# Sums of weights kept in DRAM for half of the Strassen products of a hybrid decoder layer's down-projection

## The chip, the cores and the metric

The kernel runs on one core of one Trainium2 chip. The metric is the device time of one execution in microseconds. Times are medians of several runs; a profile is one execution.

## What is computed

One decoder layer on x (256 tokens, 2048 columns, fp32): token mixing by two groups of attention heads, then a channel mixer. The change is in the channel mixer:

```python
h = rmsnorm(x, pre_ffn_g)                         # 256 x 2048
u = causal_dwconv(h @ w_up, conv_w, conv_b)       # w_up 2048 x 11264, width 3 along tokens
gate, val = jnp.split(u, 2, axis=-1)              # 256 x 5632 each
y = (gelu(gate) * val) @ w_down                   # w_down 5632 x 2048
x = x + rmsnorm(y, post_ffn_g)
```

## The kernel before

All of it is written by hand for one core. A matrix of fp32 numbers goes through TensorE (PE) in two parts: a high part (`whi`, `act.copy` on ScalarE, ACT) and a low part (`wlo`, the rest, `dve.tensor_tensor` on VectorE, DVE), and a product takes three matmuls: high x high, high x low, low x high. Weights are loaded by SP into `raw` buffers of 512 KB (five of them), split by ACT and DVE into `whi` and `wlo` (five of each), and used by PE.

The channel mixer works in two halves of the 5632 columns. For each half:

- **w_up** (`proj_T`, 11 groups g of 256 columns, gate and value): 16 matmuls high, 32 low and so on through the four units of a projection, in the order `LONG`: high of units 0 and 1, low of 0 to 3, high of 2 and 3. A `tick()` follows each of the 8 steps of a projection, 16 in a group; work put off with `later` runs at ticks. After each projection `conv` evacuates the two banks: a copy on ACT (`cs`), a sum on DVE (`u`), a product on GpSimd (POOL, `u` x `rowf`), an activation on ACT and two DVE operations, then gelu on ACT for the gate, a DVE product for the value. The result y (256 tokens of two k-tiles) is split into a tile G. For the first groups, the "sevens" below also need sums of y's quarters (`s`, on POOL, split into `sums`).
- **w_down** (four column blocks of 512, in pairs n = 0 and 2): the 22 k-tiles of the half are taken two at a time, u = 0 to 10. A **four** (`four`) is the plain product of two k-tiles and one column block for both token tiles, 12 matmuls of 512 columns; two of them cover a pair of blocks. A **seven** (`seven`) does the same 2 x 2 blocks with Strassen's seven products instead of eight, 21 matmuls in place of 24. It loads two rows of weights (`top` and `low`, 512 KB each), makes four sums of weight blocks in place on DVE (128x512 each) and four more splits. Its first three products stand before the fours of the same step, the other four (`others`) behind them; four of the seven go to banks of their own (`shared`), which `fold` adds up into y_sb after the last seven. `SEVENS` says at which steps of each half and pair sevens stand: 5, 5, 4 and 2 of them. At the end of a pair `down` evacuates the four banks of the plain products (DVE, 128x512 each).
- The last pair of half 1 (`tail`) does block 2 in its loop and block 3 in closing products: 512 columns for the first token tile, two halves of 256 columns (`b1`) for the second.

PE's instructions stand in the order of the code. Those of ACT, DVE, POOL and SP are put in order by the framework when it builds the program, by its own plan of when each can run, except where a manual schedule or `keep_in_program_order` fixes them. Each engine takes its instructions one after the other, a DMA that it issues included: a wait in front of one holds all behind it.

Lines of before that the steps touch: L119 and L122 (split of a weight unit), L263 and L270 (PE high and low of w_up), L857 to L864 (conv), L929 (gelu), L937 (gate x value), L949 to L952 (POOL's sums), L978 (products of w_down), L1005 to L1008 (a seven's weight sums), L967 (`down`), L1036 to L1050 (`fold`), L285 (`b1`).

Of the kernel before, what the change touches and what calls it, by code (L numbers as in the profile page):

```python
# [17 lines left out]
P = 128  # L18
# [9 lines left out]
SEVENS = (((0, 1, 2, 3, 4), (0, 1, 2, 3, 4)), ((0, 1, 3, 4), (0, 2)))  # L28
# [5 lines left out]
def hybrid_layer(ctx: ExitStack, tc: tile.TileContext, x, pre_mix_g, w_in, b_forget, sinks,  # L34
# [22 lines left out]

    def tick():
        now[0] += 1
        for f in todo.pop(now[0], []):  # L60
            f()
# [759 lines left out]
    with tc.tile_pool(name="ffn", bufs=1) as fp:  # L821
# [30 lines left out]
        def conv(b, ch, dst_tag):  # L852
# [6 lines left out]
            y = fp.tile([P, 256], F32, tag=dst_tag, bufs=4, name=dst_tag)  # L859
# [6 lines left out]
            return y  # L866

# [41 lines left out]
        for half in range(2):  # L909
# [3 lines left out]
            if half:  # L913
                sums = main.tile([P, 4096], F32R, tag="x", name="sums")
            for g in range(FHALF // 2):
# [10 lines left out]
                gates = []  # L926
                for m in range(2):
                    y = conv(bg[m], c0 // P + m, "yg")
                    act.activation(y, y, AF.Gelu_apprx_tanh)  # L929
                    gates.append(y)  # L930
# [4 lines left out]
                for m in range(2):  # L935
                    y = conv(bv[m], 44 + c0 // P + m, "yv")
                    dve.tensor_tensor(y, y, gates[m], op=ALU.mult)  # L937
                    ys.append(y)
                if g < most:
                    if half == 0 and g == 0:  # L940
                        for t in range(2):
                            sp.dma_start(x_dram[t * P:(t + 1) * P, :], x_sb[:, t, :])
                        sums = main.tile([P, 4096], F32R, tag="x", name="sums")
# [3 lines left out]
                    if not half:  # L947
                        s1 = a21
# [7 lines left out]
                if g < most:  # L956
                    w = 384 + 128 * half
                    split(*(sums[:, i * w:i * w + w] for i in (2 * g, 2 * g + 1)), s[:, :w])
# [31 lines left out]
            def seven(n, u, last, banks, opened):  # L990
# [3 lines left out]
                top, low = [w_load(w_rows(w_down, k + i, 1, n * 512, 1024), 1, 1024, raw=x)[0]  # L994
                            for i, x in enumerate((None, None if tail else fp.tile(
                                [P, UNIT], F32, tag="gbc", bufs=2, name="low")))]
                b11, b12, b21, b22 = (x[:, i:i + 512] for x in (top, low) for i in (0, 512))
                w = 384 + 128 * half
                s2, s3, s4, s1 = [[sums[:, v * w + i * P:v * w + i * P + P]
                                   for v in (2 * u, 2 * u + 1)] for i in range(4)]  # L1000
                if not half:
                    s1 = parts_of(u * 2, 1)
                (w11,) = split_into(w_parts(UNIT, held=False), top, 1)
                w21, w22 = split_into(w_parts(UNIT, held=False), low, 2)
                dve.tensor_tensor(b11, b12, b11, op=ALU.subtract)  # L1005
                dve.tensor_tensor(b12, b22, b12, op=ALU.subtract)
                dve.tensor_tensor(b22, b22, b11, op=ALU.subtract)
# [188 lines left out]
```

## Time and profile before

| | |
|---|---|
| Median of 3 runs | 1057.03 us (1056.82 to 1058.18) |
| The profiled execution | 1056.84 us |
| its span, first to last instruction | 1055.1 us |
| granted TensorE clock | 0.999 |
| moved by DMA | 207.09 MB, mean 196 GB/s |
| w_up, one group of two projections | 21.88 us |

In the profile PE is TensorE's matmuls and PEld its weight loads, which overlap them. L119 is line 119 of the kernel. "out<-in" names tiles without their buffer numbers. A row of a group ends in busy us, mean ns of one, and the idle time before it with what ended it. `<-issue` stands where the profile shows no releaser. SPq and ACTq are the DMAs that SP and ACT issue.

### The profile page before, as it was taken

The numbers are of one execution on the slowest core, as the hardware profiler recorded it, in microseconds if no ns is written. First come the engines' busy times: TensorE is split into PE (matmuls) and PEld (weight loads), VectorE is DVE, ScalarE is ACT, GpSimd is POOL, SyncE is SP. The second block draws the span as 40 slices with busy tenths as digits, with TensorE's granted clock in tenths as the row PEclk, the third lists the DMA queues.
The fourth block names the chain that finished last, engine by engine and source line by source line (L and its number), as shares of the span: only waits on it lengthen the run. The fifth ranks groups of instructions, "written<-read, shape, count | busy, mean of one in ns | idle before, by whom it ended". The sixth has DMA issues, their size and how long they took to land.

```text
span 1055.1 us, 16356 instructions
## 1 busy us (share of the span) xinstructions
PE 1044.0 (99%) x5914; PEld 909.2 (86%) x5914; DVE 833.1 (79%) x1337; ACT 639.8 (61%) x1099; POOL 256.2 (24%) x287
## 2 busy tenths in 40 slices
PE   9999999999999999999999999999999999999996
PEld 7889988888889888888888887888888888888886
DVE  5989877886468887887768999877778677788994
ACT  7777757767557666665655655546566565565651
POOL 3253236341122332321212000003432121200031
PEclk9999999999999999999999999999999999999999
DMA  8645666545875766656664666775657665647583
GB/s 292 194 122 180 181 188 204 176 157 161 299 239 179 228 202 198 199 182 200 199 193 149 193 204 202 239 217 183 191 173 214 199 197 184 192 147 231 175 266 125
DMA packets 161597, 207.09 MB, mean 196 GB/s; under 512 B 6860, under 2 KB 131052, under 8 KB 160620
## 3 DMA queue, kind: packets, MB, share of 16 engines
q1 hardware_dynamic: 161196, 205.65, 62.7%
q8 instruction: 46, 0.75, 0.3%
q10 hardware_dynamic: 320, 0.40, 0.1%
q14 instruction: 35, 0.29, 0.1%
HBM read 201.68 MB, written 4.21 MB: 195 GB/s over the span
## 4 chain that ended last, share of the span: by engine, by line
PE 96%; DVE 2%; DMA 1%; issue 0%; ACT 0%; SPq 0%; DVEq 0%; POOLq 0%; ACTq 0%
PE bank_acc L263 21%; PE bank_acc L978 16%; PE bank_att L263 15%; PE bank_acc L285 13%; PE bank_acc L270 11%; PE bank_att L270 8%; PE bank_att L978 4%; PE bank_att L285 1%; PE bank_att L451 1%; PE bank_att L486 1%; PE bank_att L495 1%; PE bank_acc L882 1%; PE bank_acc L226 1%; DMA x_in<-in_x_dram 1%; PE bank_att L226 1%; DVE wlo L122 0%
## 5 line engine op out<-in xcount | busy, mean ns | idle before, releaser
L122 DVE TENSOR_TENSOR wlo<-raw,whi 128x1024 fp32r<-128x1024 f32 (+3 forms) x325 | 397.6, 1238 | 110.9 <-ACT whi L119 104.6
L119 ACT CAST whi<-raw 128x1024 fp32r<-128x1024 f32 (+3 forms) x324 | 329.5, 1033 | 162.4 <-issue 82.6
L263 PE MATMUL bank_acc<-hT,whi 128*128 128x512 f32 x1024 | 245.6, 392 | 0.0
L263 PEld LDWEIGHTS bank_acc<-hT,whi 128*128 128x128 f32 x1024 | 188.2, 188 | 37.1
L858 POOL TENSOR_TENSOR u<-u,rowf 128x256 f32<-128x256 f32 x88 | 94.5, 1095 | 436.7 <-DVE u L857 433.8
L263 PE MATMUL bank_att<-hT,whi 128*128 128x512 f32 x704 | 165.7, 390 | 0.0
L263 PEld LDWEIGHTS bank_att<-hT,whi 128*128 128x128 f32 x704 | 130.6, 188 | 26.2
L978 PE MATMUL bank_acc<-whi,G 128*128 128x512 f32 x468 | 153.1, 389 | 0.0
L270 PEld LDWEIGHTS bank_acc<-hT,wlo 128*128 128x128 f32 x1024 | 123.5, 188 | 3.2
L270 PE MATMUL bank_acc<-hT,wlo 128*128 128x256 f32 x1024 | 125.8, 278 | 0.0
L978 PEld LDWEIGHTS bank_acc<-whi,G 128*128 128x128 f32 x468 | 87.9, 188 | 18.0
L978 PE MATMUL bank_acc<-wlo,G 128*128 128x512 f32 x234 | 91.3, 390 | 0.7 <-DVE wlo L122 0.7
L270 PEld LDWEIGHTS bank_att<-hT,wlo 128*128 128x128 f32 x704 | 83.6, 188 | 1.9
L270 PE MATMUL bank_att<-hT,wlo 128*128 128x256 f32 x704 | 84.0, 277 | 0.0
L285 PE MATMUL bank_acc<-whi,oT 128*128 128x512 f32 (+1 forms) x272 | 81.8, 379 | 0.0
L285 PEld LDWEIGHTS bank_acc<-whi,oT 128*128 128x128 f32 x272 | 50.2, 188 | 9.3
L978 PEld LDWEIGHTS bank_acc<-wlo,G 128*128 128x128 f32 x234 | 44.0, 188 | 10.1 <-DVE wlo L122 1.1
L285 PE MATMUL bank_acc<-wlo,oT 128*128 128x512 f32 (+1 forms) x136 | 51.3, 377 | 0.0
L860 ACT ACTIVATE yg<-u,cw 128x256 f32<-128x256 f32 x44 | 26.5, 603 | 35.6 <-POOL u L858 35.6
L285 PE MATMUL bank_acc<-whi,hT 128*128 128x384 f32 (+1 forms) x192 | 46.9, 323 | 0.0
L288 ACT CAST whi<-low 128x1024 fp32r<-128x1024 f32 x28 | 29.4, 1049 | 22.2 <-DVE low L1008 10.4
L288 ACT CAST whi<-raw 128x1024 fp32r<-128x1024 f32 (+1 forms) x36 | 31.0, 860 | 19.2 <-PE bank_acc L978 11.5
(258 smaller groups left out, 1412.6 us busy)
## 6 DMA issues: line engine op xcount, KB each, us to landing
raw<-in_w_up_dram SPq DMA_DIRECT2D x176, 512.0 KB, 4.3
raw<-in_w_down_dram SPq DMA_DIRECT2D x74, 512.0 KB, 5.0
raw<-in_w_in_dram SPq DMA_DIRECT2D x51, 512.0 KB, 5.1
raw<-in_w_out_dram SPq DMA_DIRECT2D x32, 512.0 KB, 4.5
low<-in_w_down_dram SPq DMA_DIRECT2D x14, 512.0 KB, 5.9
raw<-in_w_in_dram SPq DMA_DIRECT2D x16, 384.0 KB, 3.3
cb<-c_dram SPq DMA_DIRECT2D x8, 256.0 KB, 4.5
x_sb<-in_x_dram SPq DMA_DIRECT2D x2, 1024.0 KB, 6.4
```

Of the source, the lines that this page charges most:

```text
L119: i1 = act.copy(hi[:, cs], raw[:, cs])
L122: i2 = dve.tensor_tensor(lo[:, cs], raw[:, cs], hi[:, cs].bitcast(F32), op=ALU.subtract)
L226: pe.matmul(b, hi[:, a, m * P:(m + 1) * P], hT[:, kt, 0:512], start=(kt == 0), stop=(kt == KT - 1))
L263: pe.matmul(b, hi[:, a, m * P:(m + 1) * P], hT[:, kt, 0:512], start=(kt == 0), stop=(last == (0, kt)))
L270: pe.matmul(b[:, 256:512], lo[:, a, m * P:(m + 1) * P], hT[:, u * 4 + a, 0:256], start=False, stop=(last == (1, u * 4 + a)))
L285: pe.matmul(b, a, r[:, cols], start=(first and i == 0), stop=(last and i == 2))
L288: act.copy(hi, src)
L451: pe.matmul(sb[e][:, cs], a[r, t * P:(t + 1) * P], b[r, 0:nk], start=(n == 0), stop=(n == 2))
L486: pe.transpose(pb[:, i * P:(i + 1) * P], p[:, e, c:c + P], ident)
L858: pool.tensor_tensor(u[:, 2:258], u[:, 2:258], rowf, op=ALU.mult)
L860: act.activation(y, u[:, 2:258], AF.Identity, bias=cw[:, 3, ch:ch + 1], scale=cw[:, 2, ch:ch + 1])
L978: pe.matmul(b, x, r, start=b not in opened and not i, stop=closes and i == 2)
```

## The change

The sevens become 6, 6, 5 and 3. Two may now stand at one step: the first as before, the second whole behind the step's fours and the first one's `others`. Half of them, `STORED`, do not make their four sums of weights in w_down. `stage` makes them during w_up of the same half: in pieces of 256 columns, each loaded by two DMAs of 256 KB from w_down, summed by four DVE operations of 128x256, and stored into a DRAM tile `t_dram` with one DMA of 512 KB. The DMAs are issued from ACT. A piece is spread over 11 ticks by `staged`: load, add at the fifth tick, store at the eighth, and the next load at the twelfth. There are 12 pieces in half 0 and 10 in half 1, all through one buffer. In w_down such a seven loads the three weight blocks that it uses as they are (256 and 512 KB) and the four sums from DRAM (2 x 512 KB).

To make room, the convolution's four results of a group share one tile `yy` (two buffers), `low` takes a buffer of `yy`, the staging buffer shares one with half of the gain row (`gb0`), and the sums of y's quarters of a sixth (in half 1 a fifth) seven lie in the other's (`gb1`).

```diff
-SEVENS = (((0, 1, 2, 3, 4), (0, 1, 2, 3, 4)), ((0, 1, 3, 4), (0, 2)))
+SEVENS = (((0, 0, 1, 1, 2, 2), (0, 0, 1, 1, 2, 2)), ((0, 0, 1, 1, 2), (0, 1, 2)))
+STORED = (((1, 3, 5), (1, 3, 5)), ((1, 3), (0, 1, 2)))
...
+    staged = []
+
     def tick():
         now[0] += 1
+        f = staged.pop(0) if staged else None
+        if f:
+            f()
         for f in todo.pop(now[0], []):
             f()
...
+        def stage(half, n, u):
+
+            k = half * FHALF + u * 2
+            t = in_dram[half, n, u] = tc.dram_tile([P, 4, 512], F32, name="t_dram")
+            src = w_down[k * P:(k + 2) * P, n * 512:(n + 2) * 512].rearrange(
+                "(a p) (b c) -> p a b c", p=P, b=2)
+            for j in (slice(0, 256), slice(256, 512)):
+                b = []
+
+                def load(j=j, b=b):
+                    x = fp.tile([P, 4, 256], F32, tag="gb0", name="staged")
+                    for a in range(2):
+                        tc.keep_in_program_order(
+                            act.dma_start(x[:, 2 * a:2 * a + 2, :], src[:, a, :, j]))
+                    b.append(x)
+
+                def add(b=b):
+                    b11, b12, b21, b22 = (b[0][:, i, :] for i in range(4))
+                    for y, p, q in ((b11, b12, b11), (b12, b22, b12), (b22, b22, b11),
+                                    (b21, b21, b22)):
+                        tc.keep_in_program_order(dve.tensor_tensor(y, p, q, op=ALU.subtract))
+
+                def store(j=j, b=b):
+                    tc.keep_in_program_order(act.dma_start(t[:, :, j], b[0]))
+
+                staged.extend((load, None, None, None, add, None, None, store, None, None, None))
...
+                yy = fp.tile([P, 4, 256], F32, tag="yy", bufs=2, name="yy")
...
+                if not g:
+                    for c, us in enumerate(STORED[half]):
+                        for u in us:
+                            stage(half, 2 * c, u)
...
-                top, low = [w_load(w_rows(w_down, k + i, 1, n * 512, 1024), 1, 1024, raw=x)[0]
-                            for i, x in enumerate((None, None if tail else fp.tile(
-                                [P, UNIT], F32, tag="gbc", bufs=2, name="low")))]
+                t = in_dram.get((half, n, u))
+                if t is None:
+                    top, low = [w_load(w_rows(w_down, k + i, 1, n * 512, 1024), 1, 1024, raw=x)[0]
+                                for i, x in enumerate((None, fp.tile(
+                                    [P, UNIT], F32, tag="yy", bufs=2, name="low")))]
+                else:
+                    top = w_load(w_rows(w_down, k, 1, n * 512, 512), 1, 512)[0]
+                    low = w_load(w_rows(w_down, k + 1, 1, n * 512, 1024), 1, 1024)[0]
...
+                if t is None:
+                    b11, b12, b21, b22 = (x[:, i:i + 512] for x in (top, low) for i in (0, 512))
+                    dve.tensor_tensor(b11, b12, b11, op=ALU.subtract)
+                    dve.tensor_tensor(b12, b22, b12, op=ALU.subtract)
+                    dve.tensor_tensor(b22, b22, b11, op=ALU.subtract)
+                    dve.tensor_tensor(b21, b21, b22, op=ALU.subtract)
...
                 def others():
-                    t1, t3 = split_into(w_parts(UNIT, held=False), top, 2)
-                    t4, t2 = split_into(w_parts(UNIT, held=False), low, 2)
+                    if t is None:
+                        one, two = top, low
+                    else:
+                        one, two = [w_load(t[:, i:i + 2, :], 2, 512)[0] for i in (0, 2)]
+                    t1, t3 = split_into(w_parts(UNIT, held=False), one, 2)
+                    t4, t2 = split_into(w_parts(UNIT, held=False), two, 2)
...
-                    others = None
-                    if i in at:
-                        u = at.index(i)
-                        others = seven(n, u, u == len(at) - 1, (b, e, g, *shared), opened)
+                    here = [u for u, x in enumerate(at) if x == i]
+                    begun = [lambda u=u: seven(n, u, u == len(at) - 1, (b, e, g, *shared), opened)
+                             for u in here]
+                    others = begun[0]() if begun else None
...
                     if others:
                         others()
+                    for x in begun[1:]:
+                        x()()
```

How the order moves is shown at three places. **ACT in w_up of half 0**, from the second group's gelu (L929) over the evacuation of its value projection (`cs` of bank_att) to the casts behind. Before:

```order
L929 ACTIVATE yg<-yg 128x256 x2
L119 CAST whi<-raw 128x1024
L856 COPY cs<-bank_att 128x256 x2
L119 CAST whi<-raw 128x1024
L860 ACTIVATE yv<-u_3946,cw 128x256
L860 ACTIVATE yv<-u_3947,cw 128x256
L119 CAST whi<-raw 128x1024 x2
```

And with the change, where L976 is the gelu, L898 the store of the second piece and L888 the two loads of the third:

```order
L976 ACTIVATE yy<-yy 128x256 x2
L898 DMA t_dram<-staged 512x1x256
L125 CAST whi<-raw 128x1024
L862 COPY cs<-bank_att 128x256 x2
L888 DMA staged<-in_w_down_dram 128x2x256 x2
L865 ACTIVATE yy<-u_3946,cw 128x256
L865 ACTIVATE yy<-u_3947,cw 128x256
L125 CAST whi<-raw 128x1024 x3
```

The store has come ahead of a cast, the next loads one cast and one evacuation behind it, ahead of the convolution's activations and three casts.

**DVE just ahead of it**, from the evacuation of the second group's gate (`u` is its sum, `yg` its convolution, `wlo` the low parts of w_up's units) to that of its value. Before:

```order
L857 TENSOR_TENSOR u_3945<-bank_att,cs 128x256
L122 TENSOR_TENSOR wlo<-raw,whi 128x1024
L862 SCALAR_TENSOR_TENSOR yg<-u_3944,cw,yg 128x256
L862 SCALAR_TENSOR_TENSOR yg<-u_3945,cw,yg 128x256
L864 SCALAR_TENSOR_TENSOR yg<-u_3944,cw,yg 128x256
L864 SCALAR_TENSOR_TENSOR yg<-u_3945,cw,yg 128x256
L122 TENSOR_TENSOR wlo<-raw,whi 128x1024 x3
```

And with the change, with the second piece's four sums (L895):

```order
L895 TENSOR_TENSOR staged<-staged 128x256
L128 TENSOR_TENSOR wlo<-raw,whi 128x1024
L867 SCALAR_TENSOR_TENSOR yy<-u_3944,cw,yy 128x256
L867 SCALAR_TENSOR_TENSOR yy<-u_3945,cw,yy 128x256
L869 SCALAR_TENSOR_TENSOR yy<-u_3944,cw,yy 128x256
L869 SCALAR_TENSOR_TENSOR yy<-u_3945,cw,yy 128x256
L895 TENSOR_TENSOR staged<-staged 128x256
L128 TENSOR_TENSOR wlo<-raw,whi 128x1024
L895 TENSOR_TENSOR staged<-staged 128x256
L128 TENSOR_TENSOR wlo<-raw,whi 128x1024
L895 TENSOR_TENSOR staged<-staged 128x256
L128 TENSOR_TENSOR wlo<-raw,whi 128x1024
```

The four sums stand apart, the first ahead of the convolution, each of the others ahead of a low part.

**DVE in w_down of half 0, between its two pairs of blocks** (buffer numbers kept: `bank_att` are the banks that `fold` adds up, `bank_acc` the four that `down` evacuates). Before, L1036 to L1039 are the fold, L967 the evacuations, L1007 and L1008 the next pair's first sums of weights, L122 the low part of its first four:

```order
L289 TENSOR_TENSOR wlo_7003<-low_6994,whi_7002 128x1024
L1037 TENSOR_TENSOR y_sb_3952<-bank_att_6530,y_sb_3952 128x512
L1038 TENSOR_TENSOR y_sb_3952<-bank_att_6531,y_sb_3952 128x512
L967 TENSOR_TENSOR y_sb_3952<-bank_acc_6532,y_sb_3952 128x512
L1039 TENSOR_TENSOR y_sb_3952<-bank_att_6530,y_sb_3952 128x512
L1007 TENSOR_TENSOR low_6994<-low_6994,raw_6995 128x512
L967 TENSOR_TENSOR y_sb_3952<-bank_acc_6534,y_sb_3952 128x512
L967 TENSOR_TENSOR y_sb_3952<-bank_acc_6533,y_sb_3952 128x512
L967 TENSOR_TENSOR y_sb_3952<-bank_acc_6535,y_sb_3952 128x512
L1008 TENSOR_TENSOR low_6994<-low_6994 128x512
L122 TENSOR_TENSOR wlo_7022<-raw_7019,whi_7021 128x1024
```

With the change, L1097 is the fold's last row, L295 and L128 the low parts of the next pair's first seven and of its first two fours, L1059 to L1061 sums of that seven, L1017 the evacuations:

```order
L295 TENSOR_TENSOR wlo_7085<-raw_7081,whi_7084 128x512
L1097 TENSOR_TENSOR y_sb_3952<-bank_att_6607,y_sb_3952 128x512
L295 TENSOR_TENSOR wlo_7089<-low_7080,whi_7088 128x1024
L1059 TENSOR_TENSOR raw_7081<-raw_7081 128x512
L1060 TENSOR_TENSOR raw_7081<-low_7080,raw_7081 128x512
L128 TENSOR_TENSOR wlo_7108<-raw_7105,whi_7107 128x1024
L1017 TENSOR_TENSOR y_sb_3952<-bank_acc_6609,y_sb_3952 128x512
L1017 TENSOR_TENSOR y_sb_3952<-bank_acc_6611,y_sb_3952 128x512
L1061 TENSOR_TENSOR low_7080<-low_7080,raw_7081 128x512
L128 TENSOR_TENSOR wlo_7126<-raw_7123,whi_7125 128x1024
L1017 TENSOR_TENSOR y_sb_3952<-bank_acc_6610,y_sb_3952 128x512
L1017 TENSOR_TENSOR y_sb_3952<-bank_acc_6612,y_sb_3952 128x512
```

The first four's low part has gone ahead of all four evacuations, the second's between the two pairs of them, and the fold ahead of most of the next pair's first splits and sums.

44 lines of the change are left out of this document (23 added, 21 removed).

## Prediction

> **What bounds the kernel now.** I read the page's busy times first, then the busy time of each engine by stage, then the chain that ended last, then the timeline at two places. The first line says that TensorE (PE) has work in 99% of the span.
>
> ```profile
> PE 1044.0 (99%) x5914; PEld 909.2 (86%) x5914; DVE 833.1 (79%) x1337; ACT 639.8 (61%) x1099; POOL 256.2 (24%) x287
> ```
>
> Below are the stages of the channel mixer, one row each: w_up of half 0 from its second group on, w_down of half 0, w_up of half 1, then w_down of half 1 in its first two column blocks, and its last two up to the closing products. The columns are the stretch, its length, then busy time of PE, PEld, DVE, ACT and POOL, granted clock, DMA share and GB/s.
>
> ```profile
> 356.97:575.74 218.77, 218.77 (x1281) 193.24 (x1280) 170.78 (x250) 129.52 (x207) 58.77 (x60) 1.00 0.63 190
> 575.74:689.85 114.11, 113.39 (x500) 93.57 (x499) 105.12 (x125) 65.18 (x72) 2.22 (x2) 1.00 0.65 208
> 689.85:930.50 240.65, 240.65 (x1410) 212.55 (x1409) 182.13 (x266) 139.55 (x219) 59.70 (x58) 1.00 0.63 191
> 930.50:987.60 57.10, 57.10 (x254) 47.29 (x253) 51.90 (x65) 33.11 (x41) 2.22 (x2) 1.00 0.61 194
> 987.60:1022.60 35.00, 35.00 (x158) 29.02 (x157) 33.01 (x35) 21.27 (x26) 7.17 (x5) 1.00 0.73 233
> ```
>
> PE never waits in either w_up stage, and in w_down it lacks 0.7 us, all in half 0. So time is the count of matmuls times their pace, as long as DVE, ACT and the transfers keep ahead. DVE is nearest to not doing so: 78% busy in w_up of half 0, 76% in half 1, 91 to 94% in w_down. The pace stands in the chain of waits, 512 columns in the first row (0.2267 us each) and 256 in the second (0.120 us each):
>
> ```profile
> 576.59 6.80 PE bank_acc L978 x30
> ...
> 1038.53 8.64 PE bank_att L285 x72
> ```
>
> **The matmuls that go.** A seven is 21 matmuls of 512 where two fours are 24. There are 20 sevens for 16. Three of the new ones each save 3. The one in the last two column blocks replaces 12 of a four, 6 of the closing products of the upper tokens and 12 of 256 columns for the lower, so it adds 3 of 512 and drops 12 of 256. Together -6 x 0.2267 - 12 x 0.120 = **-2.8 us**. All of it lies on PE, which is the path.
>
> **The wait between the column blocks of half 0.** The timeline there:
>
> ```profile
> 631.67 1.88 DVE L967 TENSOR_TENSOR y_sb<-bank_acc,y_sb 128x512 f32<-128x512 f32 x3
> 633.47 0.68 DVE L1008 TENSOR_TENSOR low<-low 128x512 f32<-128x512 f32 x1
> 634.07 2.35 DVE L122 TENSOR_TENSOR wlo<-raw,whi 128x1024 fp32r<-128x1024 f32 x2
> 634.23 0.39 PE L978 MATMUL bank_acc<-whi,G 128*128 128x512 f32 x1
> 635.34 0.50 PE L978 MATMUL bank_acc<-wlo,G 128*128 128x512 f32 x1 [0.72 <-DVE wlo L122]
> ```
>
> PE's next matmul was due at 634.46 and starts at 635.34: 0.9 us lost, because DVE does four folds, four evacuations and a seven's sums before the low part of the first four. In the new order fold and evacuations stand apart: the last seven is done two rounds before the end, its fold is mixed into earlier splits, and the first four's low part stands ahead of all evacuations. The two later evacuations then end about 0.7 us after PE leaves the old block (one 0.68 row), and PE needs those banks only 6 matmuls, 1.4 us, in. I count **-0.9 us**; if the cover fails it is 0.
>
> **The staging in w_up.** 11 sevens are staged in 22 pieces, each two loads of 256 KB, four DVE sums of 128x256 and one store of 512 KB. Nothing in before does this, but each part has a near row: the DVE product of the same shape, loads of the same weights' size, stores to DRAM, and an ACT-issued DMA (issue time in ns, min/median/max). The third row is the landing of the loads of raw from 345 to 575 us.
>
> ```profile
> L937 DVE TENSOR_TENSOR yv<-yv,yg 128x256 f32<-128x256 f32 x44 | 16.6, 418 | 0.0
> raw<-in_w_up_dram SPq DMA_DIRECT2D x176, 512.0 KB, 4.3
> DMA to landing us min/median/max: 3.4/4.4/4.9
> x_dram<-x_sb SPq DMA_DIRECT2D x2, 1024.0 KB, 5.1
> out_dram<-y_sb SPq DMA_DIRECT2D x6, 256.0 KB, 2.5
> L1124 ACTq DMA_DIRECT2D out_dram<-y_sb x2: 339/351/363, 1050.0 to 1051.1; - x2
> ```
>
> DVE work: 88 x 0.418 = 36.8 us, 1.7 us a piece. A tick is a sixteenth of a group's 21.88 us, a piece takes 11 ticks, 15.0 us. DVE's free time in 15.0 us is 22% = 3.3 us in half 0 and 24% = 3.7 us in half 1, so 1.6 and 2.0 us stay free. ACT issues three DMAs, 1.05 us of 15, where it has 40% free: nothing by itself.
>
> What can cost is the waiting in ACT's queue. The store waits for the fourth sum; the next piece's loads wait until that store has landed, since there is one buffer; behind them stand the casts and the convolutions' activations, for which DVE waits. Here is one period of before, ACT first, then DVE, then PE:
>
> ```profile
> 462.15 0.72 ACT L929 ACTIVATE yg<-yg 128x256 f32<-128x256 f32 x2
> 464.78 1.05 ACT L119 CAST whi<-raw 128x1024 fp32r<-128x1024 f32 x1 [1.91 <-issue]
> 466.32 0.66 ACT L856 COPY cs<-bank_att 128x256 f32<-128x256 f32 x2 [0.49 <-PE bank_att L263]
> 468.18 0.60 ACT L860 ACTIVATE yv<-u,cw 128x256 f32<-128x256 f32 x1 [0.26 <-POOL u L858]
> ...
> 461.58 2.35 DVE L122 TENSOR_TENSOR wlo<-raw,whi 128x1024 fp32r<-128x1024 f32 x2
> 465.87 1.23 DVE L122 TENSOR_TENSOR wlo<-raw,whi 128x1024 fp32r<-128x1024 f32 x1 [1.93 <-ACT whi L119]
> 467.01 0.75 DVE L857 TENSOR_TENSOR u<-bank_att,cs 128x256 f32<-128x256 f32 x2
> ...
> 466.35 3.80 PE L263 MATMUL bank_acc<-hT,whi 128*128 128x512 f32 x16
> ```
>
> At this place of the cycle the second piece has its four sums around the two low parts that end at 463.93, so they end at 463.93 + 1.67 = 465.6. The store goes out then and ACT casts from 465.95 instead of 464.78; the low part behind ends at 468.25, not 467.1, and the sums u at 469.0. Taking 3.5 us for the store (between 2.5 for 256 KB and 5.1 for 1 MB) it lands at 469.1; two issues later, at 469.8, the activation starts that started at 468.18. DVE idles 1.4 us there and runs 1.6 us late. Late for whom: the low part of 467.1 is needed when PE, after 16 matmuls and three quarters of its low pass, comes to that unit, 466.35 + 3.65 + 2.74 = 472.7. That is 5.6 us of lead. A loss of 1.4 us in a piece is just what DVE has free (1.6 and 2.0), so it is recovered. For the first load I take 3.3 us, half the size of loads that land in 3.4 to 4.9; with the store 6.8 us, between 5.0 (two stores of 256 KB) and 10.0 (4.9 + 5.1). In the piece's 15.0 us DVE has about 6 us of sums and work among them and 8 us between, which covers 6.8 and two issues. **0 us**, with a bound below of 0, since PE waits for nothing here that could go. The bound above is the first rival's.
>
> The Trainium skill (DMA: Bandwidth & Descriptors, Anatomy of one DMA) gives a DMA 2.0 us and the bytes at 436 GB/s. An estimate by it is 3.2 us for the store and 2.6 for the load; the term would be 0 as well. The w_up load would be 3.2 by that rule and measures 4.3, so the row decides. The page also says that the receipt of a write can be surprisingly late above all in HBM, which speaks against the change; no run here shows that yet.
>
> **What w_down loads.** A stored seven loads 256 + 512 + 2 x 512 KB, 1.75 MB, where one unstored takes 1 MB. A round of two sevens and two fours is 3.93 MB in 66 x 0.2267 = 15.0 us, 263 GB/s for 208 before. In the last blocks a stored seven and a four are 2.36 MB in 7.5 us, 315 GB/s for 22 us. There 233 GB/s took a share of 0.73, so full is near 319. The loads just fit. DVE, freed of 7 x 4 sums of 0.69 us in w_down, has room to be late and catch up; PE's lead of some 5 us covers the first. I charge **+0.4 us**, between 0 and 3 (8% less rate over 22 us is 2, plus a late first load in each stage).
>
> The first seven of each w_down stage also changes its `low` buffer: it shares the convolution's, and its load moves behind five loads of raw on SP, the last of which waits for the last w_up low part:
>
> ```profile
> low<-in_w_down_dram SPq DMA_DIRECT2D x14, 512.0 KB, 5.9
> ...
> 564.33 1.22 DVE L122 TENSOR_TENSOR wlo<-raw,whi 128x1024 fp32r<-128x1024 f32 x1 [1.52 <-ACT whi L119]
> 570.25 1.21 DVE L289 TENSOR_TENSOR wlo<-low,whi 128x1024 fp32r<-128x1024 f32 x1
> 576.43 0.39 PE L978 MATMUL bank_acc<-whi,G 128*128 128x512 f32 x1
> ```
>
> Issued at 566.0 it lands by 571.9; cast, sum and split end at 574.3, and PE needs them at 576.4. Nothing; without that 2 us it would be a wait of the landing's excess. The gain row's load, which now shares the staging buffer, waits on SP in w_up of half 1 behind the last store; the loads behind it are five buffers ahead. Nothing.
>
> **Sum.** The profiled execution took 1056.84 us (span 1055.1), 0.19 under the median. 1056.84 - 2.8 - 0.9 + 0 + 0.4 = 1053.5, by the median **1053.7 us**. 0.2%, about what a measurement of this kernel can tell from no change, is 2.1 us.
>
> **Rivals.** *The staging binds w_up (slower, 0.25).* ACT waits for each store, DVE for ACT and for each load. If store and load land 1.4 us later than I took, 8.2 us in place of 6.8, DVE loses 1.4 + 1.4 us a piece against 1.8 free: 1.0 us x 22 pieces = 22, less the lead of 5.6 us in each half, makes 10.8 us; with the other terms 1064.5. At 10.0 us it is 2.8 x 22 - 11 = 51 us. It decides from about 7.6 us on, where the lead (0.5 us a piece) and the free time are used up. For it: the added transfers bring DMA from 0.63 to about 0.86 (70 GB/s more), and two w_up loads in flight already land in 4.9. POOL speaks for it as well, in two rows of one shape:
>
> ```profile
> L949 POOL TENSOR_TENSOR s<-yv 128x128 f32<-128x128 f32 x9 | 17.6, 1951 | 21.8 <-DVE yv L937 21.8
> L952 POOL TENSOR_TENSOR s<-yv,s 128x128 f32<-128x128 f32 x9 | 4.8, 535 | 0.7
> ```
>
> The first runs beside a DVE subtraction of two SBUF operands and takes 1.4 us more. The sums are such operations too; at up to 0.42 us for each convolution that meets one they make its activation later, which takes at most 1.2 us of a piece's free time and at worst moves the point of decision down to 6.4 us, under the 6.8 that I took. That is why this has 0.25 and not 0.15. The Trainium skill (SBUF — State Buffer, Who interferes with whom) has this rule: DVE with two SBUF inputs and a GpSimd operation that reads SBUF exclude each other. By it alone the sum would stay; the rows agree with it.
>
> *The transfers of w_down eat the gain (no change, 0.2).* If the last blocks get 290 GB/s and every stored seven's first t load, which waits until its round's `top` is split, is 0.2 us late, it costs 2.0 + 11 x 0.2 = 4.2 in place of 0.4: 1057.5. For it: 315 of 319; against: DVE's relief.
>
> **How the numbers follow.** My forecast has 0.55, its own range 1052.6 (no charge in w_down, 0.7 us of luck) to 1054.9 (1.2 us more of waits). Below is no mechanism. The range reaches over the second rival to the first's 1064.5 and leaves out the upper half of the first and a little below: 1052.6 to 1064.5. Faster by over 0.2% 0.55, within 0.2% 0.2, slower 0.25.
>
> **What would show it.** PE unbroken in both w_up stages with DVE near 88%; DVE waits on ACT casts of 1 to 2 us behind each load; no gap at the change of blocks in half 0; stores landing in about 3.5 us. PE waits on wlo in w_up, growing from the fourth piece on, or landings over 4 us for both, would make me wrong; so would PE waits in the last blocks of over 2 us.

## The result and the profile after

The kernel with the change takes 1083.12 us in the median of 5 runs (1082.68 to 1087.39), the one before 1057.03: a ratio of 1.0254, interval 1.0234 to 1.0273. It is 26.1 us slower. The profiled execution spans 1081.1 us, 26.0 more than before.

First the busy times from the page of after, to set beside those of before:

```profile
PE 1054.2 (98%) x5896; PEld 913.4 (84%) x5896; DVE 849.8 (79%) x1407; ACT 647.8 (60%) x1109; POOL 243.4 (23%) x295
```

PE has 18 instructions less and is busy 10 us longer, in a span that is 26 us longer: it waits, and it also runs slower. Where, the table by stage tells. Its columns are those of the table in the prediction; the stretches run from the first product of one stage to the first of the next: w_up of half 0 from its second group, w_down, w_up of half 1, w_down up to the last product. Before:

```profile
356.95:575.75 218.80, 218.80 (x1281) 193.26 (x1280) 170.79 (x250) 129.55 (x207) 58.77 (x60) 1.00 0.63 190
575.75:689.69 113.94, 113.22 (x499) 93.42 (x498) 104.95 (x124) 65.17 (x72) 2.22 (x2) 1.00 0.65 208
689.69:930.37 240.68, 240.68 (x1409) 212.58 (x1408) 182.16 (x266) 139.42 (x219) 59.70 (x58) 1.00 0.63 191
930.37:1046.88 116.51, 116.51 (x567) 98.65 (x565) 98.70 (x116) 60.22 (x78) 16.52 (x11) 1.00 0.61 199
```

And after:

```profile
357.21:591.02 233.81, 225.81 (x1281) 197.07 (x1280) 186.44 (x298) 129.79 (x208) 50.78 (x64) 0.99 0.72 229
591.02:703.12 112.10, 111.89 (x493) 92.25 (x492) 100.39 (x114) 68.46 (x76) 2.22 (x2) 1.00 0.77 255
703.12:957.81 254.69, 245.94 (x1409) 214.98 (x1408) 195.14 (x305) 140.68 (x220) 52.53 (x62) 0.99 0.70 222
957.81:1072.87 115.06, 115.06 (x555) 97.20 (x553) 91.32 (x109) 63.63 (x82) 16.65 (x11) 1.00 0.72 242
```

The two w_up stages lose 15.0 and 14.0 us, the two w_down stages gain 1.8 and 1.5. The products of w_up are the same in number (1281 and 1409). DVE is busy 15.6 us more in the first row and 13.0 in the third, yet its share of the stage is 80 and 77%: it has room and stands idle all the same. So the next view is who waited for whom. These are PE's waits (us in total, times, the longest), the two that belong to w_up:

```profile
PE bank_acc L276 <- DVE wlo L128: 10.2, 12, 2.5
PE bank_att L276 <- DVE wlo L128: 5.4, 9, 1.7
```

And these are ACT's waits that name the staging, first in half 0, then in half 1 (`DVE staged` is a store that waits for the sums, `DMA t_dram<-staged` a load that waits for the store before it to land; each is shown at the operation that stands behind it in ACT's queue):

```profile
ACT whi L125 <- DVE staged L895: 10.0, 3, 3.5
ACT yy L865 <- DMA t_dram<-staged: 9.4, 2, 5.4
ACT cs L862 <- DVE staged L895: 8.1, 3, 4.1
ACT G L294 <- DMA t_dram<-staged: 2.8, 1, 2.8
```

```profile
ACT whi L125 <- DVE staged L895: 13.3, 4, 5.1
ACT cs L862 <- DVE staged L895: 5.9, 2, 3.9
ACT yy L865 <- DMA t_dram<-staged: 1.4, 1, 1.4
```

ACT stood 30.3 us for the staging in half 0 (18.1 for sums, 12.2 for landings) and 20.6 in half 1 (19.2 and 1.4). DVE, too, stood in front of the first sum of a piece when its loads were late, in both halves together:

```profile
DVE staged L895 <- DMA staged<-in_w_down_dram: 15.1, 7, 4.0
```

One pass of it, in order of time, from the last sum of the second piece to PE:

```profile
379.15 0.41 DVE L895 TENSOR_TENSOR staged<-staged 128x256 f32<-128x256 f32 x1
379.59 0.53 ACTq L898 DMA_DIRECT2D t_dram<-staged  x1
380.24 1.05 ACT L125 CAST whi<-raw 128x1024 fp32r<-128x1024 f32 x1 [3.47 <-DVE staged L895]
386.29 0.90 ACTq L888 DMA_DIRECT2D staged<-in_w_down_dram  x2
387.23 1.09 ACT L865 ACTIVATE yy<-u,cw 128x256 f32<-128x256 f32 x2 [5.40 <-DMA t_dram<-staged]
387.86 0.48 DVE L867 SCALAR_TENSOR_TENSOR yy<-u,cw,yy 128x256 f32<-128x256 f32 x1 [4.65 <-ACT yy L865]
397.35 1.19 PE L276 MATMUL bank_acc<-hT,wlo 128*128 128x256 f32 x8 [1.68 <-DVE wlo L128]
```

The store goes out only when ACT has stood 3.5 us for the sum. The next loads go out at 386.29, when the store has landed, 6.7 us later, and the activation behind them 5.4 us late. DVE stands 4.65 us for that activation. Ten us later PE waits for a low part, in the third piece, and does so again until 498.8; the last store goes out at 548.2. In half 1 the first such wait comes at 776.4, in the fourth piece.

### The profile page after: what moved, and what is told of

Same layout as the page of the kernel before. It is cut to its first block, busy times and chain, and to the rows that moved or that the text cites. A ratio compares the mean times of both kernels' runs of the same rounds, so it can differ in the third digit from the quotient of the medians.

```text
span 1081.1 us, 16627 instructions
## 1 busy us (share of the span) xinstructions
PE 1054.2 (98%) x5896; PEld 913.4 (84%) x5896; DVE 849.8 (79%) x1407; ACT 647.8 (60%) x1109; POOL 243.4 (23%) x295
## 4 chain that ended last, share of the span: by engine, by line
PE 69%; DMA 11%; DVE 9%; issue 4%; POOL 4%; ACT 2%; ACTq 1%; SPq 0%; DVEq 0%; POOLq 0%
PE bank_acc L269 14%; PE bank_acc L291 12%; PE bank_acc L1028 12%; PE bank_att L269 8%; PE bank_acc L276 7%; DMA t_dram<-staged 6%; PE bank_att L276 4%; PE bank_att L1028 4%; DVE wlo L128 3%; DMA staged<-in_w_down_dram 3%; DMA raw<-in_w_down_dram 2%; POOL s L995 2%; DVE staged L895 2%; ACT whi L125 1%; PE bank_att L291 1%
## 5 line engine op out<-in xcount | busy, mean ns | idle before, releaser
L128 DVE TENSOR_TENSOR wlo<-raw,whi 128x1024 fp32r<-128x1024 f32 (+3 forms) x317 | 393.4, 1250 | 102.4 <-ACT whi L125 95.1
L125 ACT CAST whi<-raw 128x1024 fp32r<-128x1024 f32 (+3 forms) x316 | 321.8, 1032 | 152.1 <-issue 34.7
L864 POOL TENSOR_TENSOR u<-u,rowf 128x256 f32<-128x256 f32 x88 | 70.0, 816 | 459.3 <-DVE u L863 456.4
L1028 PE MATMUL bank_acc<-whi,G 128*128 128x512 f32 x424 | 140.1, 389 | 0.2 <-DVE y_sb L1017 0.2
L1028 PEld LDWEIGHTS bank_acc<-whi,G 128*128 128x128 f32 x424 | 79.6, 188 | 16.9 <-DVE y_sb L1017 0.6
L865 ACT ACTIVATE yy<-u,cw 128x256 f32<-128x256 f32 x88 | 52.5, 602 | 58.9 <-POOL u L864 43.2
L1028 PE MATMUL bank_acc<-wlo,G 128*128 128x512 f32 x212 | 82.6, 389 | 0.0
L295 DVE TENSOR_TENSOR wlo<-raw,whi 128x1024 fp32r<-128x1024 f32 (+1 forms) x62 | 65.0, 1071 | 10.7 <-ACT whi L294 9.6
L294 ACT CAST whi<-raw 128x1024 fp32r<-128x1024 f32 (+1 forms) x62 | 56.1, 913 | 23.4 <-PE bank_acc L1028 13.4
L867 DVE SCALAR_TENSOR_TENSOR yy<-u,cw,yy 128x256 f32<-128x256 f32 x88 | 44.6, 529 | 18.1 <-ACT yy L865 17.7
L895 DVE TENSOR_TENSOR staged<-staged 128x256 f32<-128x256 f32 x88 | 40.4, 459 | 16.0 <-DMA staged<-in_w_down_dram 15.1
```

The costliest lines, as they stand in the source:

```text
L125: i1 = act.copy(hi[:, cs], raw[:, cs])
L128: i2 = dve.tensor_tensor(lo[:, cs], raw[:, cs], hi[:, cs].bitcast(F32), op=ALU.subtract)
L294: act.copy(hi, src)
L295: dve.tensor_tensor(lo, src, hi.bitcast(F32), op=ALU.subtract)
L864: pool.tensor_tensor(u[:, 2:258], u[:, 2:258], rowf, op=ALU.mult)
L865: act.activation(y, u[:, 2:258], AF.Identity, bias=cw[:, 3, ch:ch + 1], scale=cw[:, 2, ch:ch + 1])
```

## The experiments

For each run the table gives the time, the interval of its ratio to before (taken beside it, with medians of 1056.90 to 1056.94 in these rounds), and the length of the four stages in its profile, in the order of the tables above. A profile is one execution. Those of pace, spread_sp and gb0yy_sp are the slowest of their runs (2.1, 3.2 and 1.8 us above the median) and that of late_store the fastest (2.5 below), so a difference of 1 or 2 us in a stage of these four says little; the others lie within 0.9 us of their medians.

| run | us (lowest to highest) | interval of the ratio | w_up 0 | w_down 0 | w_up 1 | w_down 1 |
|---|---|---|---|---|---|---|
| before | 1057.03 | | 218.8 | 113.9 | 240.7 | 116.5 |
| the change | 1083.12 (1082.68 to 1087.39) | 1.0234 to 1.0273 | 233.8 | 112.1 | 254.7 | 115.1 |
| four_buffers | 1073.26 (1071.62 to 1074.07) | 1.0137 to 1.0167 | 221.0 | 114.5 | 253.7 | 115.5 |
| no_sums | 1055.86 (1053.48 to 1057.14) | 0.9978 to 0.9997 | 218.8 | 114.1 | 240.7 | 115.8 |
| all_sp | 1057.14 (1055.11 to 1059.74) | 0.9993 to 1.0011 | 219.6 | 113.7 | 240.7 | 116.6 |
| all_plain | 1077.65 (1075.93 to 1078.54) | 1.0178 to 1.0208 | 218.8 | 126.0 | 240.7 | 126.1 |
| pace | 1071.02 (1068.43 to 1073.15) | 1.0112 to 1.0150 | 229.6 | 115.7 | 244.5 | 116.5 |
| late_store | 1070.99 (1068.54 to 1075.80) | 1.0111 to 1.0164 | 225.2 | 115.4 | 241.9 | 118.7 |
| loads_sp | 1067.52 (1065.21 to 1067.85) | 1.0076 to 1.0110 | 225.6 | 113.6 | 246.0 | 115.1 |
| spread_sp | 1058.28 (1056.02 to 1061.51) | 1.0004 to 1.0028 | 220.0 | 118.7 | 241.0 | 115.1 |
| one_t | 1055.18 (1054.51 to 1057.47) | 0.9976 to 0.9994 | 219.6 | 111.6 | 240.9 | 115.4 |
| gb0_sp | 1054.58 (1053.73 to 1055.65) | 0.9969 to 0.9988 | 219.7 | 111.5 | 240.7 | 115.1 |
| gb0yy_sp | 1060.97 (1059.27 to 1062.75) | 1.0021 to 1.0046 | 220.1 | 114.6 | 241.5 | 119.5 |
| four_gb0_sp | 1053.66 (1053.32 to 1054.32) | 0.9956 to 0.9981 | 218.8 | 111.5 | 240.7 | 115.5 |

The theory (A): ACT's queue. Its rivals: DVE's sums are too much work (B), the added transfers make w_up's loads late (C). In the cuts of code below "..." marks lines left out, and a comment is a note that is not in the kernel.

**all_sp: the same DMAs from another queue.**

```diff
-                            act.dma_start(x[:, 2 * a:2 * a + 2, :], src[:, a, :, j]))
+                            sp.dma_start(x[:, 2 * a:2 * a + 2, :], src[:, a, :, j]))
...
-                    tc.keep_in_program_order(act.dma_start(t[:, :, j], b[0]))
+                    tc.keep_in_program_order(sp.dma_start(t[:, :, j], b[0]))
```

> The staging's loads and stores are issued from SP in place of ACT; sums, buffer and ticks stay. Theory A: nothing stands in front of ACT's casts any more; SP stands in front of weight loads, of which five buffers are ahead; w_up of half 0 falls to 219 to 224, of half 1 to 241 to 246, the whole to 1054 to 1064 us. Rival B: w_up stays within 3 us of 233.8 and 254.7, 1080 to 1084. Rival C: the same as B.

The 29.0 us of w_up go down to 0.8 and 0.0, with all sums, loads, stores and the one buffer kept. That decides for A against B and C. One thing came along with the edit: the framework ordered ACT's and DVE's work in w_up a little otherwise (in each half some 20 of ACT's 210 to 220 places and 20 to 40 of DVE's 300 hold another instruction than in the change, mostly its neighbour). No run holds the order fixed, but loads_sp below has nearly the order of all_sp (some 10 such places on each engine in each half) and keeps 6.8 and 5.4 us of the loss, so the order by itself does not make w_up whole. The waits have not gone: now SP has them, in front of the staging's loads (L888) and stores (L898).

```profile
SPq L888 <- DMA t_dram<-staged: 48.7, 20, 5.4
SPq L898 <- DVE staged L895: 15.2, 13, 3.0
```

SP stands 48.7 us for stores to land, where ACT stood 13.6, and it costs nothing in half 1: behind it are only weight loads with five buffers ahead. The whole is at par with before and not under it, for w_down is 3.1 us longer than in the change; that is taken up below.

**no_sums: what starts the delay.**

```diff
-                staged.extend((load, None, None, None, add, None, None, store, None, None, None))
+                staged.extend((load, None, None, None, None, None, None, store, None, None, None))
```

> Leaves out the four DVE sums of every staged piece; its loads and its store stay, at the same ticks. Theory A: the store then waits in ACT's queue for the loads' landing only, which is past at its tick, and the load still waits for the store; of ACT's 30 us of standing in half 0 the 12 us in front of loads stay, so w_up keeps 4 to 9 of the 15 us and as much of the 14 in half 1, the whole is 1062 to 1072 us. Rival B: all of the loss goes, w_up takes 218.8 and 240.7, the whole 1053 to 1055. Rival C: nothing goes, 1083.

By its time alone rival B would have won: all of w_up's loss goes. Theory A had expected that the loads still wait for the stores, and was wrong in that. In this run ACT stood 1.8 us in all for landings in half 0, and nothing in half 1: a store that goes out at its tick has landed when the next load comes, 4 ticks (5.5 us) later. So in this kernel landings hold ACT almost only when the sums have made the store late. The sums are gone here, so this run by itself speaks neither for A nor against B.

**four_buffers: no load waits for a store, in half 0 only.**

```diff
...
-                    x = fp.tile([P, 4, 256], F32, tag="gb0", name="staged")
+                    if half:
+                        x = fp.tile([P, 4, 256], F32, tag="gb0", name="staged")
+                    else:
+                        x = slots[pieces[0] % 4]        # four 4 KB parts of y_sb
+                        pieces[0] += 1
```

> The staged pieces of half 0 rotate over four buffers that lie in y_sb, which is not written before w_down; half 1 keeps its single buffer and is the control. So in half 0 no load waits for the store before it. Theory A (ACT's queue: it stands in front of each store until the sums are done, and in front of each next load until the store has landed, and DVE and PE wait for the casts and activations behind): half of ACT's standing goes, the 12.2 us in front of loads in half 0, so w_up of half 0 from its second group on falls from 233.8 to between 221 and 228 us, half 1 stays at 254.7 (within 1), the whole is 1071 to 1078 us. Rival B (DVE's 1.7 us of sums a piece and what they do to POOL are the bound): both stay, 1083. Rival C (the staged transfers make the loads of w_up late): both stay, 1083.

Half 0 keeps 2.2 of its 15.0 us, half 1 is unchanged at 253.7, as A expected. But ACT's standing for sums in half 0, which A had left in place, is gone as well: with loads that go out in time the sums stand done when the store comes. So the two waits are one ring: a late store makes the next load late, the load the sums, the sums the next store. Cut at the buffer (here) or at the sums (no_sums), it opens.

**pace, late_store and loads_sp: loosening the ring.** A1 and A2 name two roots, the load that waits for the landing and the store that waits for the sums. pace leaves more ticks ahead of the next load, late_store also more ticks between sums and store, loads_sp moves the loads alone to SP.

```diff
-                staged.extend((load, None, None, None, add, None, None, store, None, None, None))
+                n_add, n_store, n_next = (4, 7, 16) if half else (4, 7, 13)     # pace
+                n_add, n_store, n_next = (5, 10, 16) if half else (4, 9, 13)    # late_store
+                staged.extend((load, *[None] * (n_add - 1), add, *[None] * (n_store - n_add - 1),
+                               store, *[None] * (n_next - n_store - 1)))
```

> All DMAs of the staging from ACT and one buffer, as in the change; load, sums and store stand at the same ticks of a piece, and only the next piece's load comes later: 6 ticks (8.2 us) behind the store in half 0, 9 ticks (12.3 us) in half 1, in place of 4 (5.5 us). Stores landed in 4.1 to 7.0 us. Theory A1 (the root is the one buffer: a load that stands in ACT's queue until the store has landed is late, and then so are its sums and the next store): w_up of half 0 falls to 219 to 224, of half 1 to 241 to 243, the whole to 1054 to 1062 us. Theory A2 (the root is the store that waits in ACT's queue for the sums, 19.2 of the 20.6 us that ACT stood for the staging in half 1): with the store at the same tick behind the sums both halves keep more than half of their loss, 226 and 248 or more, the whole 1070 or more.

> As pace, 13 ticks for a piece in half 0 and 16 in half 1, but with the store later behind the sums: 5 ticks (6.8 us) in place of 3; so the next load is 4 ticks behind the store in half 0, as in the change, and 6 in half 1. A1: half 0 keeps some of its loss, since the load still waits for the store (221 to 229), half 1 loses 0 to 1 us. A2: half 0 loses 0 to 2 us (219 to 221), half 1 as little. The whole 1054 to 1064 us by A1, 1053 to 1056 by A2.

> Only the staging's loads go to SP; the stores stay in ACT's queue and wait there for the sums. A1: no load stands before ACT's casts, and SP's waiting for a store's landing is covered by five weight buffers: w_up falls to 219 to 222 and 241 to 244, the whole to 1055 to 1061 us. A2: the stores still hold ACT for the sums: 226 and 248 or more, 1068 us or more.

Neither root holds alone. pace came out as A2 has it in half 0 and in the whole, in half 1 between the two; late_store has A1's loss in half 0, a little more in half 1, and a whole above both, with a w_down 3.7 us longer than that of before; loads_sp stands between. In loads_sp the ring is not cut: the loads still wait for the one buffer, on SP, and longer than in all_sp.

```profile
SPq L888 <- DMA t_dram<-staged: 94.5, 20, 7.9
```

Here is what ACT stood for the staging, from its waits in each profile, beside the loss of the stage:

| run and half | ticks of a piece | for sums, us | for landings, us | loss of w_up, us |
|---|---|---|---|---|
| the change, 0 | 11 | 18.1 | 12.2 | 15.0 |
| the change, 1 | 11 | 19.2 | 1.4 | 14.0 |
| pace, 0 | 13 | 18.0 | 10.7 | 10.8 |
| pace, 1 | 16 | 18.0 | 0 | 3.8 |
| late_store, 0 | 13 | 15.7 | 12.1 | 6.4 |
| late_store, 1 | 16 | 6.9 | 0 | 1.2 |
| loads_sp, 0 | 11 | 11.6 | 0 | 6.8 |
| loads_sp, 1 | 11 | 23.9 | 0 | 5.4 |

About the same standing, 18 to 21 us, cost 14 us with 11 ticks and 3.8 with 16. That DVE catches up in the added ticks would explain it, but is not shown: in pace the sums also stand at other places of DVE's order. And the standing alone does not set the loss: half 1 of loads_sp stood longest for sums, with 11 ticks, and lost 5.4 us where the change lost 14.0. Why it cost less there stays open.

**all_plain: sevens without staging.**

```diff
-STORED = (((1, 3, 5), (1, 3, 5)), ((1, 3), (0, 1, 2)))
+STORED = (((), ()), ((), ()))
```

> The sevens of the change, 6, 6, 5 and 3, but none stored and no staging: each makes its sums in w_down. All theories: w_up is as before, 218.8 and 240.7. In w_down each seven more than before brings DVE 6.9 us of sums and splits where two fours bring 2.4, so 4.5 us more for 0.68 us less of PE; in half 0 DVE had 105.1 of 114.1 us, with two more sevens 114.1 of 112.8: w_down of half 0 takes 113 to 116 where the change has 112.1. The whole 1055 to 1060 us. If it were under 1054, storing the sums would not have been needed at all.

w_up is as before, but w_down takes 126.0 us in half 0, 10 more than the most expected, and 126.1 in half 1. DVE is busy 116 of the 126 us in half 0, and PE waits for it or for casts of sums that DVE has just made. So these four more sevens do not pay while all of them make their sums in w_down.

**spread_sp, one_t, gb0_sp: why w_down is longer once w_up is whole.** In all_sp ACT has a cast that comes 2.94 us late for its weights, and 12 us later PE waits at the change of blocks of half 0:

```profile
622.05 1.05 ACT L125 CAST whi<-raw 128x1024 fp32r<-128x1024 f32 x1 [2.94 <-DMA raw<-in_w_down_dram]
```

```profile
634.21 0.47 PE L1028 MATMUL bank_acc<-whi,G 128*128 128x512 f32 x1 [0.88 <-DVE y_sb L1017]
637.05 0.50 PE L1028 MATMUL bank_acc<-whi,G 128*128 128x512 f32 x1 [0.54 <-DVE y_sb L1017]
```

The order of ACT and DVE in w_down is the one of the change, in which the same cast came 1.25 us late and PE waited 0.2. The question was whether the late weights (C2) or DVE's work at the change of blocks (D2) is the cause.

```diff
...
-SEVENS = (((0, 0, 1, 1, 2, 2), (0, 0, 1, 1, 2, 2)), ((0, 0, 1, 1, 2), (0, 1, 2)))
+SEVENS = (((0, 0, 1, 1, 2, 3), (0, 0, 1, 1, 2, 3)), ((0, 0, 1, 2, 3), (0, 1, 2)))   # spread_sp
...
-                        one, two = [w_load(t[:, i:i + 2, :], 2, 512)[0] for i in (0, 2)]
+                        one = two = w_load(t[:, 0:2, :], 2, 512)[0]                         # one_t
...
+                        one, two = [w_load(t[:, i:i + 2, :], 2, 512, raw=x)[0]              # gb0_sp
+                                    for i, x in ((0, None if tail else fp.tile(
+                                        [P, UNIT], F32, tag="gb0", name="one")), (2, None))]
```

> DMAs from SP, as in the run that issued all from there (1057.1 us; w_down 113.7 and 116.6 us up to the last product, for 112.1 and 115.1 in the change), and the sevens spread: each pair of half 0 has its last seven one step later, half 1's first pair its last two. If w_down waits for late weights because two sevens stand at each of the first steps (load C2), then both stages come near 112 and 115 and the whole to 1053 to 1055 us. If what is late is DVE at the change of blocks (D2), the fold now stands one step nearer to it, its waits grow from 1.4 to 2 or 3 us, and the whole is 1057 to 1060 us.

> DMAs from SP, as in the run that issued all from there (w_down 113.7 and 116.6 us, the whole 1057.1). Leaves out one of the two loads of sums of each stored seven and uses the other in its place, so that w_down loads 11 x 512 KB less and holds 11 buffers of weights less; every split and product stays. If what w_down has above the change's 112.1 and 115.1 us is late weights (load C2), it falls to 112 to 112.5 and 115 to 115.3, the whole to 1053.5 to 1055 us. If it is DVE's work at the change of blocks (D2), which is the same, both stay, 1057 us.

> DMAs from SP, all loads kept, and the first of a stored seven's two tiles of sums goes into the staging buffer, which stands empty in w_down, in place of a weight buffer (not in the last two blocks, where it holds the gain row). C2: loads run one buffer further ahead, the late weights in half 0 and in half 1's first pair go, w_down falls to 112 to 113 and 115 to 115.5, the whole to 1053.5 to 1055.5 us. D2: no change, 1057 us.

spread_sp splits. Half 1, whose change of blocks was not in question, falls to 115.1 with no PE wait, as C2 has it. Half 0 rises to 118.7: with the fold one step later PE waits 0.78 us for an evacuation and 1.73 for a low part at the change of blocks, as D2 has it, and then runs at half its clock for 6 us (last section). That profile is the slowest of ten runs, 3.2 us over their median, so the rise of half 0 is probably smaller in the others. one_t and gb0_sp decide for the order as the change has it: with one load less, or with one buffer more and every load kept, w_down of half 0 is 111.5 to 111.6 and of half 1 115.1 to 115.4, and PE waits in neither stage, though DVE has the same work, and ACT and DVE the same order as in all_sp. ACT's casts stood 13.6 us for weights of w_down in half 0 of all_sp, 2.9 in one_t and 3.8 in gb0_sp. So there it is C2; D2 is what a later fold would add. gb0_sp leaves out nothing and is 0.2% faster than before.

**gb0yy_sp and four_gb0_sp: how far it goes.**

```diff
+                                        (2, fp.tile([P, UNIT], F32, tag="yy", bufs=2,       # gb0yy_sp
+                                                    name="two")))]
```

> As the run before with the staging buffer, and the second tile of sums goes to the convolution's buffers, which the unstored sevens use as well. C2: two buffers further ahead, 1053 to 1055 us, unless the loads that now wait for the convolution's buffers hold up SP in w_down's first step (1056 to 1058). D2: 1057 us.

> DMAs from SP, sums in the staging buffer in w_down, and in half 0 the four staging buffers in y_sb. w_up of half 0 was 219.6 us with one buffer from SP, 0.8 above before; with four SP never stands for a store there and that goes, 218.8. By C2 the whole is 0.5 to 1 us under the run with the staging buffer alone, 1053 to 1054.5 us; by D2 1056 us.

A second buffer taken from the convolution's two, which the unstored sevens use, makes w_down 3.1 and 4.5 us longer than in gb0_sp's profile (the whole 6.4 in the medians). That is the way expected for the case that loads wait for these buffers, and more than the 1056 to 1058 us given for it; which wait decides stays open. The staging buffer in w_down together with four buffers in half 0's w_up is the fastest of all, 1053.66 us. Its stages:

```profile
356.94:575.74 218.80, 218.80 (x1281) 193.24 (x1280) 189.39 (x298) 130.60 (x208) 59.63 (x64) 1.00 0.77 246
575.74:687.26 111.52, 111.52 (x493) 92.34 (x492) 100.29 (x114) 68.91 (x76) 2.22 (x2) 1.00 0.78 255
687.26:927.94 240.68, 240.68 (x1409) 212.56 (x1408) 196.88 (x303) 139.97 (x220) 60.73 (x62) 1.00 0.74 234
927.94:1043.41 115.47, 115.41 (x555) 97.01 (x553) 92.27 (x110) 63.60 (x82) 16.65 (x11) 1.00 0.73 241
```

DVE does 18.6 us more in the first row than before and PE is unbroken. It beats gb0_sp by 0.9 us in the medians; its first row is 0.85 us shorter, its last 0.4 longer.

## Why the prediction was wrong, step by step

- **The step that failed** is the staging in w_up: 0 us, "a loss of 1.4 us in a piece is just what DVE has free (1.6 and 2.0), so it is recovered". It measured 29.0 us, 1.25 us a piece in half 0 (12 pieces) and 1.4 in half 1 (10). With the 1.6 and 2.0 us that DVE had free in a piece, an estimate of DVE's time lost is 2.9 to 3.4 us a piece, where the step had 1.4; it leaves out PE's lead.
- **Two things in that step were off.** The first is a size. The landings were taken as 3.5 us for the store and 3.3 for the first load, 6.8 together. In the page of after:

```profile
staged<-in_w_down_dram ACTq DMA_DIRECT2D x44, 256.0 KB, 4.5
t_dram<-staged ACTq DMA_DIRECT2D x22, 512.0 KB, 5.3
```

  9.8 us together (of the landings that the trace has, 17 loads and 9 stores), next to the upper bound of 10.0 and over the 7.6 from which the rival was to decide. The size alone does not make the loss: in half 0 of four_buffers and of no_sums the stores landed in 5.2 and 4.8 us (medians), the loads in 5.3 and 4.2, and that stage lost 2.2 us and nothing.
- The second is the mechanism. The step followed one store and one load, each from a punctual start. It took the store's wait for the sums as a shift of 1.2 us of one cast, and did not close the ring: DVE's sums stand behind low parts, these behind casts, the casts behind the store that waits for the sums. Measured, ACT stood up to 5.1 us at once for a sum. ACT stood longer for sums (37.3 us in both halves) than for landings (13.6).
- **The rival that the staging binds w_up** was right in kind and place, PE waiting on low parts from the third piece of half 0 and the fourth of half 1 on (the forecast said the fourth). Its 10.8 us were too few because it set 8.2 us for the landings. Its own rule would give 46 us with the measured 9.8 (3.0 over 6.8, and 1.4, against 1.8 free, is 2.6 a piece; times 22, less 11); so its size was not right either: it charged landings in every piece, and ACT met them in 4 of 22. Both signs that the prediction had named for being wrong in w_up came: PE's waits for low parts, and landings over 4 us for loads and stores.
- **The matmuls that go and the change of blocks** were right. w_down of the change gained 3.3 us where 2.8 + 0.9 less the charge of 0.4 is 3.3. That is the sum; the three terms were not measured one by one. In gb0_sp it gained 3.9, with no wait left.
- **The charge for w_down's loads**, 0.4 between 0 and 3, held in the change's own profile: 0.4, as what is left of that sum. In all_sp, at the same places of the same order, weights came later and it was 3.5, over its upper bound; why they came earlier in the change was not settled. The second rival put this price at the last two blocks; there PE waits in no run with stored sevens. The late weights stood in the first steps of half 1 and at the change of blocks in half 0, and one more buffer took PE's waits away.
- **DVE's room** was right: the sums, 40.0 us there in place of the 36.8 taken, fit into w_up of four_gb0_sp with PE unbroken.

The Trainium skill (DMA: Bandwidth & Descriptors, Anatomy of one DMA) says that a wait on a semaphore happens at the engine that issues the DMA, ahead of sending it, not in the DMA's own queue. The trace agrees: the activation behind a load stood 5.40 us. The same page's fit, which that section gives for DMAs issued by GpSimd, makes 3.2 us for the store, an estimate; 5.3 was measured here, so the measurement decides. Its remark on late receipts of writes, which the prediction put among the things against the change, is not settled: loads of the same 512 KB took 4.4 to 5.6 us (medians) in the same profile.

## What to carry to other kernels

A DMA that has to wait, for data or for its buffer, belongs in the queue of an engine behind whose wait nothing urgent stands: here the waits of the same transfers cost w_up 29 us in front of ACT's casts and under 1 us in front of weight loads with five buffers ahead (w_down then lost 3.1 us until it had one more buffer). When an engine waits for the result of another that takes its input from the first, follow the ring once around with a late start, not only with a punctual one. A gain of a few us in the last stage may also need one more buffer before it appears, so measure stage by stage.

## What the runs showed of the hardware

The granted clock fell behind PE's waits. In spread_sp PE waited 0.78 us until 636.2 and 1.73 us until 639.1. These are the stretches from there (the clock is the last column but two):

```profile
637.00:639.00 2.00, 0.35 (x2) 0.00 (x0) 2.00 (x4) 0.99 (x2) 0.00 (x0) 0.85 0.00 0
639.00:641.00 2.00, 1.92 (x5) 1.53 (x6) 2.00 (x3) 0.57 (x2) 0.00 (x0) 0.50 0.39 123
641.00:643.00 2.00, 2.00 (x6) 1.60 (x5) 2.00 (x3) 0.00 (x0) 0.00 (x0) 0.50 0.93 320
643.00:645.00 2.00, 2.00 (x6) 1.52 (x5) 0.04 (x1) 0.82 (x1) 0.00 (x0) 0.50 0.69 227
645.00:647.00 2.00, 2.00 (x9) 1.59 (x9) 1.23 (x1) 0.22 (x1) 0.00 (x0) 0.94 0.94 327
```

For 6 us PE ran at half its clock, 3 us lost over and above 2.5 us of waits: three products take 1.28 us there and 0.68 otherwise. In after it fell likewise behind the waits near 397 (1.68 and 0.74 us), 472 (1.67 and 0.28) and 837 (2.49), and stayed at 1.00 behind groups of waits of 0.27 to 1.36 us each. One of the falls in after:

```profile
474.00:476.00 2.00, 2.00 (x9) 1.96 (x10) 1.48 (x3) 2.00 (x4) 1.24 (x2) 0.56 0.92 266
476.00:478.00 2.00, 2.00 (x7) 1.56 (x6) 2.00 (x5) 0.20 (x1) 0.00 (x0) 0.59 1.06 368
```

In half 0 of after the two groups with a fall, at 0.94 over the 26.4 us from 379.1 on and 0.93 over the 26.1 us up to 480.2, make 3.4 of the 15.0 us; 8.0 are idle time of PE, and the other 3.6, in which PE counts as busy, are not accounted for. So waits of about 2 us in all can cost more than themselves. It is no sharp rule: in loads_sp the clock fell to 0.50 behind waits of 1.17 and 0.74 us (until 801.6 and 803.6) and stayed at 1.00 behind 0.73 and 1.20 (until 441.4 and 443.8). The Trainium skill (TensorE: Matmul & The Clock Gate, Part 1) puts the fall behind an idle window of about 3.4 us; here, in the falls of after, PE stood still for 1.9 to 2.5 us in all, so the measurement decides. The relation was seen in the traces and not tried by itself.

The DMA rate is not capped at the 319 GB/s that the prediction inferred from a share: the last row above has 368, over 2 us.
